# Hybrid decoder trunk on one core: more background steps between gates, row sums and their matmuls, finer steps in the S5 set-up, and four PSUM copies put first

## The chip, the cores and the metric

The kernel runs on one core of one Trainium2 chip. The metric is the device time of one execution in microseconds (us), lower is better. The core has a matrix engine (PE, with weight loads as a row of their own, PEld), a vector engine (DVE), a scalar engine (ACT), a general engine (POOL) and a queue engine that issues most transfers (SP). Each works through its own list of instructions in order, and semaphores hold an instruction until what it needs is there.

## What is computed

One layer: a wide input projection, three token mixers on parts of its columns, an output projection, and a layer norm over the residual. All is float32, 1024 tokens of width 2048.

```python
h = jnp.einsum('bld,dn->bln', x, w_in[l])
(s5_u, s5_z, ml_qk, ml_v, ml_i, ml_f, ml_o, ml_z, ssd_xbc, ssd_dt, ssd_z) = split_in(h)
y_s5 = s5_mixer(s5_u, ...) * jax.nn.silu(s5_z)
qk = jax.nn.silu(causal_dwconv(ml_qk, ml_conv_w[l], ml_conv_b[l]))
q, k = jnp.split(qk, 2, axis=-1)
y_ml = mlstm_mixer(q, k, ml_v, ml_i + ml_i_bias[l], ml_f + ml_f_bias[l], ml_o, ml_norm_g[l]) * jax.nn.silu(ml_z)
xbc = jax.nn.silu(causal_dwconv(ssd_xbc, ssd_conv_w[l], ssd_conv_b[l]))
xs, bs, cs = jnp.split(xbc, [SSD_WIDTH, SSD_WIDTH + SSD_GROUPS * SSD_STATE], axis=-1)
y = ssd_mixer(xs, bs, cs, ssd_dt, ssd_dt_bias[l], ssd_a_log[l], ssd_d[l])
y_ssd = rms_norm(y * jax.nn.silu(ssd_z), ssd_norm_g[l])
out = jnp.einsum('bln,nd->bld', jnp.concatenate([y_s5, y_ml, y_ssd], axis=-1), w_out[l])
x = layer_norm(DEEPNORM_ALPHA * x + out, ln_g[l], ln_b[l])
```

The mixers are an S5 state space model (32 groups of 64 complex states), an mLSTM with 4 heads, and a Mamba-2 SSD with 12 heads.

## The kernel before

**Matmuls.** Every float32 product of the projections is made of three passes: each operand is split (`split`, lines 170 to 172) into a high part, cast by ACT, and the rest, subtracted by DVE; PE then multiplies high by high, high by low and low by high into one PSUM bank. A weight block is called w0, w1, ... in the order of use; the class `Weights` loads the next block, and splits it, one block ahead of its use.

**Stages.** `block()` (lines 1284 to 1456) makes the columns that need no convolution, with a Strassen scheme of seven products: first the token-major products (84 units of 24 matmuls, in the stages (1), (2), (5,6), (3,7), (4)), then 35 column-major ones, then the S5 gate. Its evacuations add products up on DVE and apply Sigmoid and Silu on ACT (`put_t`, lines 1254 to 1273). Then `half(h)` runs for tokens 0 to 511 and 512 to 1023: six tiles `qk`, seven tiles `xbc` of the first SSD group pair, three more, and four last ones that are computed side by side in four PSUM banks over eight weight blocks (lines 1518 to 1535). A tile of `qk` or `xbc` is 48 matmuls in two weight blocks (`proj_c`, lines 290 to 303). Each finished tile goes through `conv` (lines 353 to 362): ACT copies the PSUM bank into a staging tile (two buffers), POOL handles the three tokens of halo, DVE makes four multiply-adds, ACT applies Silu. `outproj(h)` follows for both halves, with four PSUM banks per block of 512 columns.

**Background.** All other work is written as Python generators that stand in one queue, `Background` (lines 138 to 165). The projection loops call `bg.tick()` after each weight block; a tick adds the rate of the generator at the head of the queue to an account, and for each whole unit in it the generator is run on to its next `yield`. So a `yield` more means a step more until what follows it is written into the program, and a rate of 2.0 means two steps per tick. `bg.finish(gen)` runs a generator to its end at once. The generators that the change touches:

- `s5_setup` (lines 749 to 1028), the constants of the S5 mixer, spread over the 84 units of the token-major stage at 0.31 steps per tick, and 0.46 from stage (3,7) on (line 1408). Its loop over eight `sb` makes `lb` and `ob` (six DVE operations), then `ta` (three) and, for the `sb` before, `read_out`: four transposes and a few small matmuls on PE, a copy on ACT.
- `pre` in `half` (lines 1484 to 1493): `gates` (some 20 small DVE operations and an Exp), `cumulate` (lines 393 to 415: 14 small matmuls of `LC` with a triangle or the identity, and four ACT copies), then `ml_gates` (lines 584 to 610: a scan over time on DVE, two row transfers, transposes `mt` on PE).
- `ssd_finish` (lines 558 to 581): products with the gate, squares and their sum `sm`, a matmul `ms` of `sm` with a matrix of 1/768, the root, and the results to DRAM.
- `ml_mix`, `ml_finish` and `ssd_super` are not edited, but stand in the queue behind `pre`. The second SSD pair and `ssd_finish` of half 0 run in half 1, ahead of that half's `pre`; those of half 1 run in the output projection of half 0.

**Order on an engine.** The program is not issued in the order in which it is written. The framework plans it once when the kernel is built: among the instructions that its own model of time holds for ready, an engine takes the one written first, and `tc.high_priority()` lets an instruction pass for one written earlier. So later work moves ahead into what the plan takes for idle time; on the chip the planned order of each engine is fixed.

Of the kernel before, what the change touches and what calls it, by code (L numbers as in the profile page):

```python
# [39 lines left out]
def hybrid_trunk(ctx: ExitStack, tc: tile.TileContext, a: dict, out: bass.AP, dbg=None):  # L40
    nc = tc.nc
    pe, act, dve, pool, sync = nc.tensor, nc.scalar, nc.vector, nc.gpsimd, nc.sync
# [13 lines left out]
    def gt(name, shape=(P, HT), dtype=F32):  # L56
        return gp.tile(list(shape), dtype, name=name, tag="g")

    def pm(name):
        return mx.tile([P, HT], F32, name=name, tag="mx")  # L60
# [34 lines left out]
    cw_s, cb_s = col("ssd_conv_w", 14), col("ssd_conv_b")  # L95
# [254 lines left out]
            bg.tick()  # L350


    def conv(ps, halo, cw, cb, t, dest, nm):
        stg = sp.tile([P, 3 + HT], F32, name=nm + "st", tag="cst")
        act.copy(out=stg[:, 3:], in_=ps)
        pool.tensor_copy(out=stg[:, 0:3], in_=halo[:, t, :])
        pool.tensor_copy(out=halo[:, t, :], in_=stg[:, HT:HT + 3])
        c = gt(nm + "cv")
        dve.tensor_scalar(out=c, in0=stg[:, 0:HT], scalar1=cw[:, t, 0:1], scalar2=cb[:, t:t + 1], op0=ALU.mult, op1=ALU.add)
        for j in range(1, 4):  # L360
            dve.scalar_tensor_tensor(out=c, in0=stg[:, j:j + HT], scalar=cw[:, t, j:j + 1], in1=c, op0=ALU.mult, op1=ALU.add)  # L361
        act.activation(out=dest, in_=c, func=AF.Silu)  # L362
# [195 lines left out]
    def ssd_finish(h, yg):  # L558
        sm = gt(f"sm{h}")
        for t in range(6):  # L560
            z = gt(f"szs{h}{t}")
            sync.dma_start(out=z, in_=szd[t * P:(t + 1) * P, h * HT:(h + 1) * HT])
            dve.tensor_mul(out=yg[t], in0=yg[t], in1=z)
            act.activation(out=z if t else sm, in_=yg[t], func=AF.Square)
            if t:
                dve.tensor_add(out=sm, in0=sm, in1=z)
            if t % 2:
                yield
        yield
        ps = pm(f"ms{h}")  # L570
        pe.matmul(ps, lhsT=ones, rhs=sm, start=True, stop=True)
        rs = gt(f"rs{h}")
        dve.tensor_scalar_add(rs, ps, EPS)
        act.activation(out=rs, in_=rs, func=AF.Sqrt)
        dve.reciprocal(rs, rs)
        yield
        for t in range(6):
            dve.scalar_tensor_tensor(out=yg[t], in0=yg[t], scalar=sg_col[:, t:t + 1], in1=rs, op0=ALU.mult, op1=ALU.mult)
            sync.dma_start(out=mixT[1280 + t * P:1280 + (t + 1) * P, h * HT:(h + 1) * HT], in_=yg[t])
            if t % 2:  # L580
                yield


    def ml_gates(h, G, NC, b, lf, ir, res):
        n = f"mg{h}"

        m = gt(n + "m", (4, HT))
        dve.tensor_tensor_scan(out=m, data0=lf, data1=ir, initial=mcar, op0=ALU.add, op1=ALU.max)
        mst = sp.tile([4, 4], F32, name=n + "mst", tag="mst")
        pool.tensor_copy(out=mst[:, 0:1], in_=mcar)  # L590
        pool.tensor_copy(out=mst[:, 1:4], in_=m[:, P - 1:3 * P:P])
        pool.tensor_copy(out=mcar, in_=m[:, HT - 1:HT])
        A = gt(n + "A", (4, HT))
        dve.tensor_tensor(out=A, in0=b, in1=m, op=ALU.subtract)
        sync.dma_start(out=rowd[h][12:16], in_=A)
        A2 = gt(n + "A2", (4, HT))
        ms = mst.unsqueeze(2).to_broadcast([4, 4, P])
        dve.tensor_tensor(out=A2.rearrange("p (c k) -> p c k", k=P), in0=A.rearrange("p (c k) -> p c k", k=P), in1=ms, op=ALU.add)
        sync.dma_start(out=rowd[h][16:20], in_=A2)

        Bj = sp.tile([P, 4, 4], F32, name=n + "Bj", tag="mBj")
        dve.tensor_tensor(out=Bj, in0=G[:, :, 16:20], in1=NC[:, :, 32:36], op=ALU.add)
        yield
        yield
        mt = pm(n + "mt")
        for c in range(4):
            pe.transpose(mt[:, 4 * c:4 * c + 4], m[:, c * P:(c + 1) * P], ident[0:4, 0:4])
        em = sp.tile([P, 16], F32, name=n + "em", tag="mem")
        act.activation(out=em, in_=mt[:, 0:16], func=AF.Exp, scale=-1.0)
        res += [Bj, em]  # L610
# [138 lines left out]
    def s5_setup():  # L749
# [28 lines left out]
        def tt(o, i, j, op, eng=dve):  # L778
            eng.tensor_tensor(out=o, in0=i, in1=j, op=op)  # L779
# [219 lines left out]
        for sb in range(8):  # L999
            g4 = slice(4 * sb, 4 * sb + 4)  # L1000
            sh = [P, 4, 8, 16]

            pv = lambda t_, lo: t_[:, lo:lo + 8, g4].rearrange("p s g -> p g s").unsqueeze(3).to_broadcast(sh)
            bv = lambda t_: t_[:, g4, :].unsqueeze(2).to_broadcast(sh)
            lb, l2 = gt(f"s5lb{sb}", sh), gt(f"s5l2{sb}", sh)
            tt(lb, pv(pdr, 1), bv(bb1), mul)
            tt(l2, pv(pds, 1), bv(bb2), mul)
            tt(lb, lb, l2, sub)
            ob, o2 = gt(f"s5ob{sb}", sh), gt(f"s5o2{sb}", sh)
            tt(ob, pv(pdr, 0), bv(c1s), mul)  # L1010
            tt(o2, pv(pdi, 0), bv(c2), mul)
            tt(ob, ob, o2, sub)
            sync.dma_start(out=s5d["O"][sb], in_=f3(ob))
            lbs[sb] = lb
            yield

            av = lambda t_: t_[:, :, g4].rearrange("p x g -> p g x").unsqueeze(3).to_broadcast(sh)
            fv = lambda t_: t_[:, :, g4].rearrange("p y g -> p g y").unsqueeze(2).to_broadcast(sh)
            ta, tb = gt(f"s5ta{sb}", sh), gt(f"s5tb{sb}", sh)
            tt(ta, av(afr), fv(f1), mul)  # L1020
            tt(tb, av(a2), fv(f2_), mul)
            tt(ta, ta, tb, add)
            sync.dma_start(out=s5d["T"][sb], in_=f3(ta))
            if sb:
                read_out(sb - 1)
            yield
# [257 lines left out]
    def block():  # L1284
# [116 lines left out]
        for sg in STAGES:  # L1401
            if sg == (2,):
                aside.append(aside_2(ops[5]))
            if sg == (5, 6):
                aside.append(aside_3())
            if sg == (3, 7):
                aside.append(aside_4())
                bg.q = [(q, 0.46) for q, _ in bg.q]
            for g in range(3):
                if sg == (5, 6):  # L1410
                    ps = {5: banks(5, g, pj), 6: banks(6, g, mx)}
                    for u in range(4):
                        w = [W.next(), W.next()]
                        for i, w_ in zip(sg, w):
                            unit(i, ops[i], g, u, ps[i], w_)
                        ahead(sg, g, 6, u)
                else:
                    for i in sg:
                        ps = banks(i, g, pj)
                        for u in range(4):  # L1420
                            if (i, g) == (1, 0):
                                first.load(u)
                            unit(i, ops[i], g, u, ps, W.next())
                            ahead(sg, g, i, u)
                if sg == (1,) and g == 0:
                    aside.append(aside_1())
# [52 lines left out]
    def half(h, X, Xn):  # L1479
# [4 lines left out]
        def pre():  # L1484
            G = Gs[:, h]
            DT, LC = gates(h, G)
            yield
            yield
            NC, b, lf, ir = cumulate(h, LC)
            gx.extend([DT, NC])  # L1490
            yield
            yield from ml_gates(h, G, NC, b, lf, ir, mlg)
        bg.add(pre(), 1.5)
        qT = [gt(f"qT{h}{i}", (96, HT)) for i in range(4)]
        kT = [gt(f"kT{h}{i}", (96, HT)) for i in range(4)]
        for t in range(6):
# [3 lines left out]
            relay(qT if t < 3 else kT, dst, t % 3)  # L1500
            bg.tick()

        def finish_conv(ps, t):
            dst = gt(f"xc{h}_{t}")
            conv(ps, halo_s, cw_s, cb_s, t, dst, f"xb{h}{t}")
            return dst

        def xbc(ts):
# [14 lines left out]
        for u in range(8):  # L1523
            wh, wl = W.next()
            order = [(q, k) for q in range(4) for k in range(2)] if u in (0, 7) else [(q, k) for k in range(2) for q in range(4)]
            for q, k in order:
                K, sl = 2 * u + k, slice(q * P, (q + 1) * P)
                x_h, x_l = X.h[u][:, k, :], X.l[u][:, k, :]
                pe.matmul(ps[q], lhsT=wh[:, k, sl], rhs=x_h, start=(K == 0), stop=False)
                pe.matmul(ps[q], lhsT=wh[:, k, sl], rhs=x_l, start=False, stop=False)  # L1530
                pe.matmul(ps[q], lhsT=wl[:, k, sl], rhs=x_h, start=False, stop=(K == 15))  # L1531
                if K == 15:
                    tiles.append(finish_conv(ps[q], ts[q]))
            Xn.load(u)
            bg.tick()
        bg.finish(mix)
# [182 lines left out]
```

## Time and profile before

| | |
|---|---|
| time before, median of 3 runs | 1612.53 us (1611.51 to 1612.76) |
| the profiled execution's own time | 1610.04 us |
| its span, first to last instruction | 1608.3 us |
| DVE busy | 1120.7 us (70%) |
| ACT busy | 658.2 us (41%) |
| POOL busy | 80.3 us (5%) |
| granted PE clock, mean | 0.994 |

Times inside the trace count from the first instruction of the profiled execution. A row of a timeline gives start, duration, engine, line, operation, what is written and read, and in brackets the idle time of the engine before it with what ended it. Matmuls overlap in the pipe: a row's duration is longer than the distance to the next row, and the distance is what a matmul costs in a full stream. So PE can be shown as busy and still lose time; where that matters, starts are compared.

### The profile page before, as it was taken

The numbers are of one execution on the slowest core, as the hardware profiler recorded it, in microseconds if no ns is written. First come the engines' busy times: TensorE is split into PE (matmuls) and PEld (weight loads), VectorE is DVE, ScalarE is ACT, GpSimd is POOL, SyncE is SP. The second block draws the span as 40 slices with busy tenths as digits, with TensorE's granted clock in tenths as the row PEclk, the third lists the DMA queues.
The fourth block names the chain that finished last, engine by engine and source line by source line (L and its number), as shares of the span: only waits on it lengthen the run. The fifth ranks groups of instructions, "written<-read, shape, count | busy, mean of one in ns | idle before, by whom it ended". The sixth has DMA issues, their size and how long they took to land. (4 is left out here: it accounts for less than half of the span.)

```text
span 1608.3 us, 21146 instructions
## 1 busy us (share of the span) xinstructions
PE 1579.1 (98%) x7688; PEld 1329.4 (83%) x7688; DVE 1120.7 (70%) x1844; ACT 658.2 (41%) x927; POOL 80.3 (5%) x183
## 2 busy tenths in 40 slices
PE   9999999999999999999999999999999999999996
PEld 7898988987988888778888888788887888888884
DVE  5678978878868786565646788685697753484348
ACT  4333242147345556543542546364354331321222
POOL 0000000000001110001100000010000000000000
PEclk9999999999999999999999999999999999999998
DMA  8988777987987768364434553452654453575345
GB/s 318 328 320 316 255 269 251 306 293 223 336 302 248 247 227 275 130 223 127 137 105 159 183 169 119 151 171 66 217 195 145 132 194 118 183 242 160 129 144 183
DMA packets 139304, 333.56 MB, mean 207 GB/s; under 512 B 24489, under 2 KB 41001, under 8 KB 139201
## 3 DMA queue, kind: packets, MB, share of 16 engines
q1 hardware_dynamic: 129792, 317.54, 59.1%
q10 hardware_dynamic: 9408, 14.68, 2.6%
q8 instruction: 60, 0.98, 0.2%
q14 instruction: 44, 0.35, 0.1%
HBM read 271.74 MB, written 57.28 MB: 205 GB/s over the span
## 5 line engine op out<-in xcount | busy, mean ns | idle before, releaser
L1297 DVE TENSOR_TENSOR e<-e,b 128x512 f32<-128x512 f32 (+1 forms) x72 | 43.9, 645 | 3.7 <-PE b L1372 3.2
L1556 DVE SCALAR_TENSOR_TENSOR r<-r,mv,ln_g 128x512 f32<-128x512 f32 x32 | 23.1, 742 | 0.0
L1557 DVE SCALAR_TENSOR_TENSOR r<-r,lrs,ln_b 128x512 f32<-128x512 f32 x32 | 23.0, 742 | 0.0
L1576 DVE BATCH_NORM_STATS2 bst<-r 128x6 f32<-128x512 f32 x32 | 20.8, 682 | 0.0
L362 ACT ACT_TABLE_LOAD x15 | 19.2, 1283 | 3.7 <-DVE qc00cv L361 3.4
L1052 POOL COPY s5m0up<-s5m0u 128x256 f32<-128x256 f32 x2 | 0.8, 398 | 316.2 <-DMA s5m0u<-s5u 316.2
L1297 DVE TENSOR_TENSOR f<-f,b1c 128x512 f32<-128x512 f32 x15 | 9.4, 682 | 8.7 <-ACT f L1350 8.7
L172 DVE TENSOR_TENSOR y1l<-y1r,y1h 128x1024 fp32r<-128x1024 f32 x8 | 9.8, 1222 | 7.5 <-ACT y1h L171 7.5
L1277 ACT ACTIVATE f<-f 128x512 f32<-128x512 f32 x20 | 12.1, 628 | 6.2 <-DVE f L1297 3.2
L171 ACT CAST y1h<-y1r 128x1024 fp32r<-128x1024 f32 x8 | 8.4, 1053 | 9.1 <-PE op03p L344 9.1
L779 DVE TENSOR_TENSOR s5small<-s5small 128x32 f32<-128x32 f32 (+2 forms) x66 | 11.2, 195 | 0.7
L1548 ACT ACTIVATE lrs<-lrs 128x1 f32<-128x1 f32 x8 | 1.6, 202 | 24.4 <-DVE lrs L1547 24.4
L1297 DVE TENSOR_TENSOR f<-f,b2c 128x512 f32<-128x512 f32 x5 | 3.4, 687 | 11.6 <-PE b2c L1444 11.6
L172 DVE TENSOR_TENSOR y0l<-y0r,y0h 128x1024 fp32r<-128x1024 f32 x8 | 9.8, 1221 | 2.3 <-ACT y0h L171 2.2
L172 DVE TENSOR_TENSOR x1l<-x1r,x1h 128x1024 fp32r<-128x1024 f32 x8 | 9.8, 1219 | 2.3 <-ACT x1h L171 2.3
L731 DVE TENSOR_TENSOR sgo<-sgo,mzs 128x384 f32<-128x384 f32 x16 | 8.9, 555 | 2.3 <-DMA mzs<-zg 2.1
L171 ACT CAST y0h<-y0r 128x1024 fp32r<-128x1024 f32 x8 | 8.4, 1046 | 4.9 <-PE xbc_13p L1531 4.8
L1271 ACT ACT_TABLE_LOAD x8 | 10.3, 1283 | 0.1
L1270 ACT ACT_TABLE_LOAD x7 | 9.0, 1283 | 2.4 <-ACT e L1271 2.4
L1305 ACT COPY e<-b 128x512 f32<-128x512 f32 (+1 forms) x12 | 6.7, 558 | 7.5 <-PE b L1372 7.5
L1160 DVE TENSOR_TENSOR gsg<-gsg,gsz 128x512 f32<-128x512 f32 x8 | 5.5, 683 | 6.0 <-DMA gsz<-s5z 6.0
L741 PEld LDWEIGHTS mf<-ident,sgo 128*128 128x128 f32 x48 | 5.7, 140 | 4.7 <-DVE sgo L731 3.8
(4696 smaller groups left out, 5741.1 us busy)
## 6 DMA issues: line engine op xcount, KB each, us to landing
xn<-in_x_dram SPq DMA_DIRECT2D x32, 256.0 KB, 5.5
out_dram<-r SPq DMA_DIRECT2D x32, 256.0 KB, 3.8
x1r<-in_xT_dram SPq DMA_DIRECT2D x8, 512.0 KB, 4.3
y0r<-mixT SPq DMA_DIRECT2D x8, 512.0 KB, 3.3
y1r<-mixT SPq DMA_DIRECT2D x8, 512.0 KB, 3.5
vd<-e SPq DMA_DIRECT2D x16, 192.0 KB, 4.0
szd<-f ACTq DMA_DIRECT2D x12, 256.0 KB, 3.0
vx<-vd SPq DMA_DIRECT2D x8, 384.0 KB, 4.3
```

What stands on the lines that cost most here:

```text
L171: act.copy(out=th, in_=raw)
L172: dve.tensor_sub(out=tl, in0=raw, in1=th.bitcast(F32))
L362: act.activation(out=dest, in_=c, func=AF.Silu)
L731: dve.tensor_mul(out=sg, in0=sg, in1=sz)
L779: eng.tensor_tensor(out=o, in0=i, in1=j, op=op)
L1270: act.activation(out=c[:, 0:256], in_=c[:, 0:256], func=AF.Silu)
L1271: act.activation(out=c[:, 256:512], in_=c[:, 256:512], func=AF.Sigmoid)
L1277: act.activation(out=c, in_=c, func=AF.Silu)
L1297: dve.tensor_tensor(out=o, in0=x, in1=y, op=op)
L1556: dve.scalar_tensor_tensor(out=o, in0=o, scalar=mv[:, 0:1], in1=lng[nb], op0=ALU.subtract, op1=ALU.mult)
L1557: dve.scalar_tensor_tensor(out=o, in0=o, scalar=rs, in1=lnb[nb], op0=ALU.mult, op1=ALU.add)
L1576: dve.bn_stats(out=st[t][:, nb, :], in_=r[t][nb])
```

## The change

`conv` can put its PSUM copy first, and does so for the last four tiles of a half. `ssd_finish` has two more yields between the sum of squares and the matmul `ms`; `ml_gates` one more after the row transfers; `pre` five instead of two between `gates` and `cumulate`, at a rate of 1.8 instead of 1.5. The loop of `s5_setup` yields four times per `sb` instead of twice, and runs at 0.95 instead of 0.46 steps per tick from stage (3,7) on.

```diff
-    def conv(ps, halo, cw, cb, t, dest, nm):
+    def conv(ps, halo, cw, cb, t, dest, nm, soon=False):
         stg = sp.tile([P, 3 + HT], F32, name=nm + "st", tag="cst")
-        act.copy(out=stg[:, 3:], in_=ps)
+        with tc.high_priority() if soon else nullcontext():
+            act.copy(out=stg[:, 3:], in_=ps)
         pool.tensor_copy(out=stg[:, 0:3], in_=halo[:, t, :])
...
             if t % 2:
                 yield
         yield
+        yield
+        yield
         ps = pm(f"ms{h}")
         pe.matmul(ps, lhsT=ones, rhs=sm, start=True, stop=True)
...
         sync.dma_start(out=rowd[h][16:20], in_=A2)
+        yield

         Bj = sp.tile([P, 4, 4], F32, name=n + "Bj", tag="mBj")
...
             tt(lb, lb, l2, sub)
+            yield
             ob, o2 = gt(f"s5ob{sb}", sh), gt(f"s5o2{sb}", sh)
             tt(ob, pv(pdr, 0), bv(c1s), mul)
...
             sync.dma_start(out=s5d["T"][sb], in_=f3(ta))
+            yield
             if sb:
                 read_out(sb - 1)
             yield
...
             if sg == (3, 7):
                 aside.append(aside_4())
-                bg.q = [(q, 0.46) for q, _ in bg.q]
+                bg.q = [(q, 0.95) for q, _ in bg.q]
...
             DT, LC = gates(h, G)
-            yield
-            yield
+            for _ in range(5):
+                yield
             NC, b, lf, ir = cumulate(h, LC)
             gx.extend([DT, NC])
             yield
             yield from ml_gates(h, G, NC, b, lf, ir, mlg)
-        bg.add(pre(), 1.5)
+        bg.add(pre(), 1.8)
...
-        def finish_conv(ps, t):
+        def finish_conv(ps, t, soon=False):
             dst = gt(f"xc{h}_{t}")
-            conv(ps, halo_s, cw_s, cb_s, t, dst, f"xb{h}{t}")
+            conv(ps, halo_s, cw_s, cb_s, t, dst, f"xb{h}{t}", soon)
             return dst
...
                 if K == 15:
-                    tiles.append(finish_conv(ps[q], ts[q]))
+                    tiles.append(finish_conv(ps[q], ts[q], True))
             Xn.load(u)
```

## The prediction, made before the changed kernel ran

> **What bounds the kernel now.** I read the page first, then the waits of PE, then the clock and the instructions around each wait.
>
> ```profile
> span 1608.3 us, 21146 instructions
> PE 1579.1 (98%) x7688; PEld 1329.4 (83%) x7688; DVE 1120.7 (70%) x1844; ACT 658.2 (41%) x927; POOL 80.3 (5%) x183
> ```
>
> PE is the bound: 98% busy, so 1608.3 - 1579.1 = 29 us of the span are without it. The change touches no matmul of the projections, so all it can give is time in which PE waits, and all it can cost is new waits. PE's waits, longest first:
>
> ```profile
> PE cu0cs L397 <- DVE gt1f L378: 1.9, 1, 1.9
> PE b L1370 <- ACT w70h L171: 1.8, 1, 1.8
> PE b L1371 <- DVE w70l L172: 1.7, 1, 1.7
> ...
> PE ms L571 <- DVE sm L566: 1.2, 1, 1.2
> PE op00p L343 <- ACT xb113st L355: 1.1, 1, 1.1
> ...
> PE mg0mt L607 <- DVE mg0m L588: 0.3, 1, 0.3
> ```
>
> Each edit has its wait here: the steps in `pre` that of cu0cs, the S5 set-up the two of w70, `ssd_finish` that of ms, the early copies that of op00p, the step in `ml_gates` that of mg0mt. Together 8.0 us. One of them costs more than its wait:
>
> ```profile
> 367.50:371.00 3.50, 1.76 (x14) 1.46 (x13) 2.23 (x4) 3.09 (x6) 0.00 (x0) 1.00 0.34 115
> 371.00:371.70 0.70, 0.62 (x3) 0.53 (x4) 0.70 (x2) 0.70 (x2) 0.00 (x0) 1.00 0.93 181
> 371.80:372.60 0.80, 0.78 (x3) 0.05 (x1) 0.80 (x2) 0.80 (x2) 0.00 (x0) 0.50 1.12 323
> 374.20:378.00 3.80, 3.74 (x9) 2.97 (x10) 3.80 (x6) 0.58 (x1) 0.00 (x0) 0.50 0.81 258
> 378.00:380.00 2.00, 2.00 (x9) 1.63 (x8) 2.00 (x3) 0.00 (x0) 0.00 (x0) 0.85 1.00 287
> 1340.00:1360.00 20.00, 20.00 (x90) 16.54 (x89) 4.00 (x4) 4.22 (x4) 0.00 (x0) 1.00 0.32 106
> ```
>
> These are windows: length, then PE, PEld, DVE, ACT and POOL busy, the granted clock, DMA. An undisturbed window holds 90 matmuls in 20 us, a step of 0.22 to 0.23 us. After 3.5 us in which PE was busy for 1.76, the clock falls to 0.50 from 371.7 until about 378.6 (0.85 over the last 2 us is 0.6 us at half), some 6.9 us. Half of that is lost, less what is waited anyway. So the w70 place costs 1.8 + 1.7 and, in the 6.9 - 1.7 us of half speed, 2.6 more: 6.1 us.
>
> **The steps in `pre`.**
>
> ```profile
> 707.91 0.39 PE L300 MATMUL qk_0p<-p23h,w124l 128*128 128x512 f32 x1
> 709.88 0.20 DVE L389 TENSOR_TENSOR gt0LC<-gt0DT,nega 128x48 f32<-128x48 f32 x1
> 710.19 0.48 PE L397 MATMUL cu0cs<-gt0LC,tri 128*128 128x144 f32 x2 [1.89 <-DVE gt1f L378]
> ```
>
> cu0cs stands right behind tile qk_0, and its input LC is finished by DVE only at 710.08. Start to start 2.28 us, less a step of 0.23: 2.05 lost. The old queue runs `gates` at the first tick of the half and `cumulate` at the second. The new one, at 1.8 and with five yields, reaches `cumulate` at the fourth, behind tile qk_1: 48 matmuls of 0.227 = 10.9 us later. LC is then ready by far, and qk_1 fills PE meanwhile, its weights being loaded. I take the whole 2.05. At worst (the plan pulls cu0cs forward again, as it pulled the other half's gates forward: gt1f at 710 belongs to half 1) it is 0. Hidden from the end: the mLSTM in half 0 starts at the thirteenth tick either way.
>
> **The step in `ml_gates`.** `cumulate` and the transposes mt stand two ticks apart before (second and fourth) and after (fourth and sixth); between them come the same ACT copies behind the same Silu of a `qk` tile. I take 0 of the 0.3; the whole of it at best.
>
> **The S5 set-up.** From stage (3,7) on the loop made two steps of 0.46 per tick and now makes four at 0.95, so it runs equally fast: one `sb` in 4.3 ticks against 4.2, no step moved by more than two ticks, and it still ends before its stage. What changes is which DVE operations stand together at w70:
>
> ```profile
> 354.44 0.42 ACT L1270 ACTIVATE e<-e 128x256 f32<-128x256 f32 x1 [2.34 <-issue]
> ...
> 367.73 0.42 ACT L1271 ACTIVATE e<-e 128x256 f32<-128x256 f32 x1
> ...
> 369.98 1.05 ACT L171 CAST w70h<-w70r 128x1024 fp32r<-128x1024 f32 x1
> ```
>
> ```profile
> 370.65 0.69 DVE L779 TENSOR_TENSOR s5l<-s5small,s5bb 128x512 f32<-128x512 f32 x1
> 371.25 0.69 DVE L779 TENSOR_TENSOR s5ob<-s5small,s5c1s 128x512 f32<-128x512 f32 x1
> 371.86 1.22 DVE L172 TENSOR_TENSOR p43l<-p43r,p43h 128x1024 fp32r<-128x1024 f32 x1
> 372.99 1.22 DVE L172 TENSOR_TENSOR w70l<-w70r,w70h 128x1024 fp32r<-128x1024 f32 x1
> ```
>
> The first wait is ACT's: eight activations with a table load between each two, 354.44 to 368.15, stand ahead of the cast w70h, which ends at 371.03. The change edits none of that. The second is DVE's: the split w70l stands behind s5l and s5ob. With a yield between `lb` and `ob`, s5ob is written one tick later and falls behind the splits; w70l starts 371.86 - 371.25 = 0.61 earlier. I take 0.61. The clock fell at 371.7, ahead of the second wait (372.6), so the first one alone brought it, and I leave the 2.6 us. Ends: 6.1 gained if the first wait goes; as much lost if such a place arises once more.
>
> **The row sums.**
>
> ```profile
> 1042.22 1.10 PE L571 MATMUL ms<-sm,ones 128*128 128x512 f32 x2 [1.23 <-DVE sm L566]
> 1306.38 0.39 PE L344 MATMUL op01p<-w214l,y0h 128*128 128x512 f32 x1
> 1306.86 1.10 PE L571 MATMUL ms<-sm,ones 128*128 128x512 f32 x2
> ```
>
> Half 0: two more steps at a rate of 2.0 are one tick. ms was written behind the first weight block of qk_5 and is now written behind the second. But in the trace it ran 22 matmuls into xbc_0 (it lies between matmuls of that tile), later than either place: the plan held it until it thought sm ready, 1.2 us too early. That error stays; I take 0, between -1.2 and +1.2. Half 1: 0.48 start to start less 0.23 is 0.25; ms there gets a tick more distance from its last squares, and I take 0.25.
>
> **The copies put first.**
>
> ```profile
> 1227.17 1.28 ACT L362 ACT_TABLE_LOAD   x1
> ...
> 1232.70 0.63 ACT L362 ACTIVATE xc<-xb19cv 128x512 f32<-128x512 f32 x1 [3.14 <-DVE xb19cv L361]
> 1233.24 0.57 ACT L355 COPY xb113st<-xbc_13p 128x512 f32<-128x512 f32 x1
> 1230.35 2.32 DVE L361 SCALAR_TENSOR_TENSOR xb19cv<-xb19st,cols,xb19cv 128x512 f32<-128x512 f32 x3
> 1233.86 0.50 PE L343 MATMUL op00p<-w203h,y0h 128*128 128x512 f32 x1 [1.12 <-ACT xb113st L355]
> ```
>
> PE waits for the fourth bank, emptied by the copy of xb113 at 1233.24. There are two staging tiles, so this fourth copy needs the second one, free when DVE ends xb19cv at 1232.67. Going first, the copy passes only the Silu: 1232.70 instead of 1233.24, 0.54 us. The rest is DVE's and stays. In half 0 no bank is waited for at this place: 0.
>
> **Sum:** 2.05 + 0 + 0.61 + 0.25 + 0.54 = 3.45 us. The profiled execution took 1610.04 (span 1608.3), which gives 1606.6 for it; the median 1612.53 lies 2.5 above, and the forecast is 1612.53 - 3.45 = **1609.1**.
>
> **Rivals.**
>
> *The clock stays up.* If readouts or copies of the set-up move so that w70h comes early enough, both waits and the half clock go: 6.1 instead of 0.61, 1609.1 - 5.5 = 1603.6. For it: finer pieces around just this place, the readout copies among them. Against: the eight activations alone end at 368.15, later than PE's last matmul of w69.
>
> *The waits only move.* From the first altered step on, the whole plan is made anew. Each wait in the list is the plan's error against the chip by 1 to 2 us, and two or three new ones eat 3.45: 1612.5, give or take 2.
>
> *Slower: the passage from half 1 to the output projection.* The queue of half 1 gets later: one tick from `ssd_finish`, and `pre` needs ten steps at 1.8 (5.6 ticks) where it needed six at 1.5 (4 ticks). Counted through, `ml_mix` starts three ticks later, `ml_finish` and the second `ssd_super` two, that is 11 us, since a tile of 10.9 us has two ticks.
>
> ```profile
> 1224.72 1.09 PE L508 MATMUL s10y<-s10A,s10dx 128*64 128x128 f32 x16
> ...
> 1228.37 0.50 PE L343 MATMUL op00p<-w203h,y0h 128*128 128x512 f32 x1
> ```
>
> Now 1228.37 - 1224.72 = 3.65 us of SSD matmuls cover the convolutions between the last `xbc` matmul and op00. Two ticks later they stand inside op00: PE needs the fourth bank at 1233.86 - 1.12 - 3.65 = 1229.1 and gets it at 1233.3, a wait of 4.2 us in place of 1.1, and the clock halves, which cost 2.6 at w70. That is 3.1 + 2.6 = 5.7 more, against 2.9 gained elsewhere: 1615.3. It decides once PE runs dry for about 1.8 us, as at w70. For it: the cover goes by count. Against: the plan sees a full bank and may put the same SSD matmuls, if ready, into the gap. An early copy could add to it, since ACT's order is fixed (3.14 us idle above, in front of a Silu) and what stands behind a copy that waits for its staging tile waits too.
>
> The Trainium skill (TensorE: Matmul & The Clock Gate, Part 1) says that the clock is halved after at least one idle window of about 3.4 us. By that rule a wait of 1.8 us, such as the one before 371.08, would not halve it, and the passage would cost its wait alone, some 1612.7. The row of 367.5 to 371 speaks against it: PE was busy for half of that stretch, with the transposes of a readout among it, and the clock fell all the same. No run here shows where the limit lies.
>
> **How the numbers follow.** Forecast 0.42 (1607 to 1611: the copy's 0.54 and the 0.61 may fail, the 1.2 of ms may go); clock up 0.18 (1602 to 1605); waits moved 0.22 (1610.5 to 1614.5); slower 0.18 (1614 to 1618). A difference of 0.2%, 3.2 us, is about what a measurement of this kernel can tell from none, so faster means below 1609.3: 0.25 of the forecast and 0.18 make 0.43; same gets 0.17 + 0.20 = 0.37; slower 0.20. Range 1602 to 1615.5: it holds the first three cases and part of the fourth.
>
> **What would show it.** Right: no wait at cu0cs, with `cumulate` behind qk_1; the Silu chain still ahead of w70h, clock at 0.50 for one stretch near 372; ms in half 0 still waiting for sm; the fourth copy in front of a Silu and ending by DVE's staging release. Wrong: a granted clock of 1.00 throughout after the start, or a second stretch of 0.50, at 1225 to 1240 above all, or waits of PE for a staging copy in the last `xbc` tiles of half 1.

## The result, and the profile after

The changed kernel takes **1620.65 us** (median of 7 runs, 1616.5 to 1627.16); the kernel before took 1611.51 on the same chip (7 runs, 1610.3 to 1613.04). The ratio is 1.0061, 95% interval 1.0039 to 1.0082: slower, and above the forecast range. The profiled execution is the median one, 1620.65 us.

The head of the page of the changed kernel:

```profile
span 1618.9 us, 21166 instructions
...
PE 1579.1 (98%) x7688; PEld 1330.6 (82%) x7688; DVE 1121.7 (69%) x1844; ACT 661.9 (41%) x929; POOL 87.9 (5%) x183
```

PE is busy for as long as before, 1579.1 us, and the span is 10.6 us longer: PE stands still for that much more. PE's waits in the changed kernel (engine, instruction, what released it: total, times, longest):

```profile
PE s5m6U L1064 <- POOL s5m5X L1092: 6.1, 1, 6.1
PE mf L745 <- DVE sgo L735: 3.5, 5, 1.0
PE b L1377 <- DVE w74l L172: 2.7, 1, 2.7
PE b L1377 <- DVE w70l L172: 2.0, 1, 2.0
PE ms L574 <- DVE sm L567: 1.9, 1, 1.9
PE b L1376 <- ACT w70h L171: 1.7, 1, 1.7
...
PE op00p L343 <- ACT xb113st L356: 0.9, 1, 0.9
```

cu0cs and mg0mt are gone from the list, as forecast for the one, and as the best case for the other. Both waits of w70 are still there. But three waits are new or much longer: s5m6U, the transposes of the S5 batch s5m6 (none before); w74l, the split of weight block w74 (0.2 before); and mf, the transposes of `ml_finish` (0.3 before). That of ms rose from 1.2 to 1.9. The first is the largest of the whole kernel, and the clock falls to half within it. The same stretches by the windows, first after, then before (length, PE, PEld, DVE, ACT, POOL busy, granted clock, DMA share, GB/s):

```profile
577.00:583.00 6.00, 0.00 (x0) 0.00 (x0) 5.44 (x7) 2.09 (x2) 5.67 (x3) 0.71 0.83 285
583.00:587.00 4.00, 3.90 (x13) 3.30 (x14) 0.00 (x0) 0.69 (x2) 1.42 (x6) 0.58 0.50 138
```

```profile
577.00:583.00 6.00, 6.00 (x31) 4.93 (x31) 6.00 (x7) 3.08 (x4) 0.97 (x2) 1.00 0.62 181
583.00:587.00 4.00, 4.00 (x27) 3.48 (x26) 3.86 (x7) 1.80 (x4) 0.11 (x1) 1.00 0.95 341
```

Six microseconds without a matmul, then 13 matmuls where 27 had run.

To set runs beside one another I add up **lost time**: the distance from the start of one matmul to the start of the next, less the median distance for that shape in the kernel before. It holds waits and half clock alike. The table gives, for one profiled execution of each kernel, what was lost in a stretch of the span beyond the kernel before:

| stretch (us) | after | set-up only | gates only | sums only | copies only | after, fraction kept | before, fraction 0.27 |
|---|---|---|---|---|---|---|---|
| w70 and w74 (360 to 415) | +2.6 | +3.9 | +0.2 | +0.2 | +0.5 | +4.9 | +1.6 |
| S5 mixing, with s5m6U (415 to 700) | +7.6 | +3.1 | 0.0 | +0.7 | +0.1 | +0.3 | +8.5 |
| gates and s01 (700 to 745, 910 to 1010) | -4.8 | -0.1 | -4.6 | -1.1 | +0.9 | -4.9 | -1.3 |
| mf, half 0 (745 to 910) | +1.6 | +0.7 | +1.0 | +0.1 | -0.1 | +1.2 | 0.0 |
| ms, half 0 (1010 to 1080) | +1.3 | -0.2 | +0.2 | +0.3 | +4.8 | +1.0 | +0.1 |
| mf, half 1 (1080 to 1205) | +3.4 | +0.3 | -0.6 | +2.0 | +0.5 | +1.7 | +0.4 |
| op00 (1205 to 1260) | -0.5 | +0.2 | -0.5 | +0.1 | -1.2 | +0.1 | -0.7 |

The stretches are wide enough that a shift of 10 us between kernels moves no such place out of its row. The column "after" adds up to 11.2 us, against 10.6 of the span; the small rest lies at both ends. Each column is one execution, and executions differ: in the kernels "gates only", "sums only", "copies only" and "before, fraction 0.27", PE's order is that of the kernel before up to 467 us or further, and yet the row of w70 reads +0.2 to +1.6 there, and the time ahead of 360 us, which is not in the table, +1.4 to +3.1. So a difference of 1 to 2 us in one cell proves nothing by itself.

**How s5m6U came to wait.** SP's timeline of the changed kernel (start, duration, engine, line, what is loaded), and that of the kernel before:

```profile
561.53 0.33 SPq L209 DMA_DIRECT2D w104r<-cg  x1
569.80 0.33 SPq L209 DMA_DIRECT2D w104q<-in_w_c_dram  x1
571.54 0.32 SPq L209 DMA_DIRECT2D w105r<-cg  x1
571.91 0.98 SPq L1055 DMA_DIRECT2D s5m6u<-s5u  x2
```

```profile
558.57 0.33 SPq L209 DMA_DIRECT2D w104r<-cg  x1
558.94 0.98 SPq L1049 DMA_DIRECT2D s5m6u<-s5u  x2
568.66 0.34 SPq L209 DMA_DIRECT2D w104q<-in_w_c_dram  x1
```

SP issues in a fixed order, and w104q waits some 8 us there for its buffer. The input of the S5 batch s5m6 stood in front of it; now it stands behind it and behind w105r, and is issued 13 us later (3 of these are the whole stretch, since w104r goes out 3 us later as well). Its consumer is a pair of copies on GpSimd. They are the second half of the story. Tile s5m6u in the changed kernel (durations min, median, max in ns; first and last start), and VectorE's timeline around them:

```profile
L1058 POOL COPY s5m6up<-s5m6u x2: 398/2884/5371, 577.3 to 582.6; 128x256 f32<-128x256 f32 x2
```

```profile
577.15 1.21 DVE L223 TENSOR_TENSOR w104r<-w104r,w104q 128x1024 f32<-128x1024 f32 x1
...
581.23 1.22 DVE L172 TENSOR_TENSOR w103l<-w101r,w103h 128x1024 fp32r<-128x1024 f32 x1
587.13 1.28 DVE L1303 TENSOR_TENSOR f<-f,b37c 128x512 f32<-128x512 f32 x2 [4.69 <-PE b37c L1450]
```

Of two equal copies one shows 0.40 us and the other 5.37. VectorE ran six two-input operations without a gap, from 577.15 to 581.23 + 1.22 = 582.45. The first copy, begun at 577.33, ended 0.25 us behind that row, and the second then took its 0.40. (The wait list names the memset s5m5X as the releaser; it stands right behind the copies on GpSimd and ended at 583.08.) The Trainium skill (SBUF — State Buffer, SBUF: two separate sides) says that GpSimd shares a port pair with VectorE, held for a whole instruction by an operation with two SBUF inputs, so that the other blocks. The trace agrees, and shows more: the copy lasted over a row of instructions, not over one.

### The profile page after: what moved, and what is told of

The parts are those of the page before. It is cut to its first block, busy times and chain, and to the rows that moved or that the text cites. A ratio compares the mean times of both kernels' runs of the same rounds, so it can differ in the third digit from the quotient of the medians.

```text
span 1618.9 us, 21166 instructions
## 1 busy us (share of the span) xinstructions
PE 1579.1 (98%) x7688; PEld 1330.6 (82%) x7688; DVE 1121.7 (69%) x1844; ACT 661.9 (41%) x929; POOL 87.9 (5%) x183
## 4 chain that ended last, share of the span: by engine, by line
PE 83%; DVE 8%; DMA 4%; issue 2%; ACT 1%; SPq 1%; DVEq 0%; POOL 0%; ACTq 0%
PE b L1377 8%; PE b L1378 8%; PE b L1376 8%; PE op01p L343 1%; PE op01p L344 1%; PE op12p L345 1%; PE op12p L343 1%; PE op11p L343 1%; PE op10p L344 1%; PE op10p L343 1%; PE op03p L344 1%; PE op03p L343 1%; PE op02p L344 1%; PE op02p L343 1%; PE op11p L345 1%
## 5 line engine op out<-in xcount | busy, mean ns | idle before, releaser
L745 PE MATMUL mf<-ident,sgo 128*128 128x128 f32 x48 | 8.8, 282 | 4.3 <-DVE sgo L735 3.5
L783 DVE TENSOR_TENSOR s5small<-s5small 128x32 f32<-128x32 f32 (+2 forms) x66 | 11.2, 194 | 0.7
L1303 DVE TENSOR_TENSOR f<-f,b37c 128x512 f32<-128x512 f32 x10 | 6.5, 678 | 5.8 <-PE b37c L1450 5.8
L171 ACT CAST x1h<-x1r 128x1024 fp32r<-128x1024 f32 x8 | 8.3, 1044 | 5.1 <-PE xbc_13p L1537 5.0
```

Source lines behind the costliest of these rows:

```text
L171: act.copy(out=th, in_=raw)
L1303: dve.tensor_tensor(out=o, in0=x, in1=y, op=op)
```

## The experiments

Two pairs of theories came up one after the other, and the names in the expectations are these. First: **A**, the set-up edits cost; **B**, the later queue of half 1 costs. Then, for the set-up: **P**, the phase of the step counter, against **T**, the stage itself; for the row sums and copies: **C** and **S**.

### The parts by themselves

Each kernel is the one before with some of the diff's hunks. The set-up only:

```diff
             tt(lb, lb, l2, sub)
+            yield
...
             sync.dma_start(out=s5d["T"][sb], in_=f3(ta))
+            yield
...
-                bg.q = [(q, 0.46) for q, _ in bg.q]
+                bg.q = [(q, 0.95) for q, _ in bg.q]
```

> Only the two yields in the S5 set-up loop and the rate 0.95; the halves as before. Theory A (the loss is made in the first stages: the set-up edits rearrange the plan there, and a transfer of the S5 mixer, s5m6u, falls behind two weight loads): the two places of after come back, a wait of PE of some 6 us at s5m6U near 577 with a second stretch of half clock, and 2.7 us at w74; waits of before in the halves unchanged. From the lost time by place in the two traces, +2.5 around w70 and w74 and +7.4 between 500 and 600 us: 9 to 10 us slower than before, about 1621. Theory B (the later queue of half 1 is what costs): no more than 2 to 3 us slower, and no wait of 6 us.

Every other hunk:

> All of the change but the S5 set-up edits. Theory A: 1608 to 1613, the gate wait (2.0) and the one at mg0mt (0.4) gone, the waits of mf in half 1 (3.3) and of ms (0.7) there as in after, so that it is within 3 us of before; no second stretch of half clock. Theory B: most of the loss is here, 1616 to 1621, from waits at mf, ms and the passage to the output projection.

The gates only:

```diff
-            yield
-            yield
+            for _ in range(5):
+                yield
...
-        bg.add(pre(), 1.5)
+        bg.add(pre(), 1.8)
...
         sync.dma_start(out=rowd[h][16:20], in_=A2)
+        yield
```

> Only the steps in pre, its rate, and the step in ml_gates. Both theories: the waits at cu0cs and mg0mt go, 2.5 us. Theory A: half 1 is later by one to two ticks, small waits at mf of up to 2 us; 1609 to 1611. Theory B: slower than before by 2 us or more.

The row sums and the copies:

```diff
         yield
+        yield
+        yield
         ps = pm(f"ms{h}")
...
-                    tiles.append(finish_conv(ps[q], ts[q]))
+                    tiles.append(finish_conv(ps[q], ts[q], True))
```

> Only the two steps in ssd_finish and the four copies put first. My prediction's step: ms in half 0 still waits for sm by 1 to 2 us, the fourth copy is about 0.5 us earlier. Both theories: within 1.5 us of before, 1610 to 1613; if the queue of half 1, one tick later here, is what makes the waits at mf, they show here too, up to 2 us.

| kernel | median us | ratio to before, 95% interval |
|---|---|---|
| set-up only | 1620.46 | 1.0041 (1.0028 to 1.0053) |
| all but set-up | 1613.56 | 0.9999 (0.9989 to 1.0008) |
| gates only | 1610.54 | 0.9978 (0.9967 to 0.9990) |
| sums and copies | 1619.32 | 1.0027 (1.0016 to 1.0039) |

By these ratios the set-up costs 0.0041 x 1613 = 6.6 us, sums and copies cost 4.4, and the gates give 3.5. Together that is +7.5, and the whole change shows +9.8, within the intervals. (The other division, set-up and all but set-up, adds up to +6.5.) So the gates' step did what it was to do, and there are two separate losses. Theory A is right on the set-up, but priced it too high: 9 to 10 us were expected of it alone.

### The set-up: a fraction left in a counter

The loop's steps are given out by a counter:

```
            self.acc += self.q[0][1]
            while self.acc >= 1.0 and self.q:
                self.acc -= 1.0
```

What is left in `acc` when the set-up ends is carried into the S5 mixing. Adding up the ticks gives 0.58 with the rate 0.46 and 0.27 with 0.95. With 0.27 the step that loads s5m6u falls one tick later. Two kernels put this to the test, one line each. In the changed kernel:

```diff
         bg.finish(setup)
+        bg.acc = 0.58
```

> The whole change, with the step counter's fraction at the end of the set-up put back to the 0.58 that it had before (the finer set-up at the new rate leaves 0.27). Theory P (phase): the set-up edits cost what they do through that fraction, since it writes the load of s5m6u one tick later, behind two weight loads on SP. With 0.58 the load stands in front of w104q again, the 6.1 us wait at s5m6U and the second half-clock stretch go: 5 to 8 us less than the changed kernel's 1620.65, so 1613 to 1616. Rival T (the stage itself): the loss is made in stage (3,7), at w70 and w74, and what follows is the clock's: the time stays at 1618.5 or more.

In the kernel before:

```diff
         bg.finish(setup)
+        bg.acc = 0.27
```

> The kernel before, with one line: the step counter's fraction set to 0.27 behind the set-up, where it was 0.58. Nothing of the change is in it. Theory P: s5m6u's load falls behind w104q and w105r as in the changed kernel, a wait of 3 us or more comes up at s5m6U, and the time rises by 3 to 7 us, to 1615 to 1619. Rival T: the order of that load does not matter, the time stays within 1.5 us of the kernel before.

The changed kernel with the old fraction took 1614.71 us (1.0011, 1.0000 to 1.0023), 6 us less by the medians, and 8 less by the ratios, which compare each kernel with the kernel before of its own session. The kernel before with the new fraction and nothing else took 1619.79 (1.0043, 1.0030 to 1.0057): 6.9 us more. Its largest wait, and SP's order, are those of the changed kernel:

```profile
PE s5m6U L1058 <- POOL s5m5X L1086: 6.1, 1, 6.1
```

```profile
572.48 0.33 SPq L209 DMA_DIRECT2D w104q<-in_w_c_dram  x1
574.22 0.32 SPq L209 DMA_DIRECT2D w105r<-cg  x1
574.59 0.98 SPq L1049 DMA_DIRECT2D s5m6u<-s5u  x2
```

Theory P holds, from both sides: this largest loss has nothing to do with what the finer steps contain.

What the late load costs at its own place depends on what VectorE does beside the copies. The kernel with the set-up only has SP's new order too, and a wait of 6 us was expected of it; it waited 3.3 us and kept the full clock there. VectorE's row broke off there at 582.50, for want of a load:

```profile
583.07 1.23 DVE L223 TENSOR_TENSOR w105r<-w105r,w105q 128x1024 f32<-128x1024 f32 x1 [0.57 <-DMA w105q<-in_w_c_dram]
```

The first copy on GpSimd, begun at 580.54, took 2.22 us and ended inside this gap.

Is it the late load, or the copies that VectorE holds up? In the changed kernel, the two copies of s5m6 went to ScalarE:

```diff
-            pool.tensor_copy(out=up.rearrange("p (g s c) -> p g s c", g=4, s=8)[:, :, 4 * i:4 * i + 4, :],
+            (act.copy if n == "s5m6" else pool.tensor_copy)(out=up.rearrange("p (g s c) -> p g s c", g=4, s=8)[:, :, 4 * i:4 * i + 4, :],
```

> The whole change, but the two copies s5m6up (GpSimd: 0.40 and 5.37 us in the changed kernel, beside an unbroken row of VectorE's two-input additions) and the two of s5m7up, which read the same load, no: only those of s5m6 are done by ScalarE; SP's order is the changed kernel's, with s5m6u late. Theory K (GpSimd's copy is held up by VectorE): the two copies take about 1.3 us together on ScalarE, the wait at s5m6U falls from 6.1 to 3.5 us or less, and 2 to 5 us of the 1620.65 go. Rival L (the load alone is late): the wait at s5m6U stays above 5 us and the time within 1.5 us of the changed kernel's.

```profile
L1058 ACT COPY s5m6up<-s5m6u x2: 404/404/404, 582.9 to 583.6; 128x256 f32<-128x256 f32 x2
```

```profile
PE b L1377 <- DVE w74l L172: 2.6, 1, 2.6
...
PE s5m6U L1064 <- ACT s5m6up L1058: 1.5, 1, 1.5
```

The wait at s5m6U fell from 6.1 to 1.5 and no half clock followed there, as theory K said. Beside ScalarE's copies, too, VectorE ran a row without a gap, until 584.39. But the time did not fall: 1620.87 us (4 runs, 1.0052, 1.0038 to 1.0065), against 2 to 5 us less expected. In the profiled execution 4.9 us less were lost at s5m6U, but 2.7 more at w74 (6.83 us of half clock behind its wait, none in the changed kernel's profile), 1.2 more at w70 and 1.4 more at op00. PE came to the transposes 5.6 us later than in the changed kernel (2.7 of them from w74), and the load went out 5.4 us later, so the two stand to each other nearly as before: by an estimate from this run, some 1.5 us of the wait belong to the late load, and the rest to the copies on GpSimd. What that is worth in the whole time it does not show.

At **w70**, where the prediction looked, VectorE's order in the changed kernel is what it was, s5ob and then the splits:

```profile
370.48 0.68 DVE L783 TENSOR_TENSOR s5ob<-s5small,s5c1s 128x512 f32<-128x512 f32 x1
...
372.22 1.22 DVE L172 TENSOR_TENSOR w70l<-w70r,w70h 128x1024 fp32r<-128x1024 f32 x1
```

The other loss in the set-up's own stage is at **w74**. VectorE's timeline and SP's row of w78q, after and then before:

```profile
400.93 1.00 DVE L223 TENSOR_TENSOR w78r<-w78r,w78q 128x808 f32<-128x808 f32 x1 [4.47 <-DMA w78q<-in_w_gv_dram]
401.85 1.22 DVE L172 TENSOR_TENSOR w74l<-w74r,w74h 128x1024 fp32r<-128x1024 f32 x1
395.88 0.33 SPq L209 DMA_DIRECT2D w78q<-in_w_gv_dram  x1
```

```profile
399.01 1.00 DVE L223 TENSOR_TENSOR w78r<-w78r,w78q 128x808 f32<-128x808 f32 x1 [1.74 <-DMA w78q<-in_w_gv_dram]
399.93 1.22 DVE L172 TENSOR_TENSOR w74l<-w74r,w74h 128x1024 fp32r<-128x1024 f32 x1
394.47 0.33 SPq L209 DMA_DIRECT2D w78q<-in_w_gv_dram  x1
```

The split w74l stands behind w78r's addition, and that waits for the load w78q. In both kernels the load is issued 0.03 us after VectorE has ended w77r's addition. In the changed kernel the products s5ta and s5tb stand ahead of that addition, it starts at 394.85 instead of 393.45, the load goes out 1.4 us later, and VectorE stands still for 4.47 us, for the last two of them with the split ready behind it. The wait grew by 2.5 us: besides the 1.4, the load itself took 0.5 longer, and PE was there 0.6 earlier. To tell steps from rate I ran the steps alone:

```diff
             tt(lb, lb, l2, sub)
+            yield
...
             sync.dma_start(out=s5d["T"][sb], in_=f3(ta))
+            yield
```

> The two further steps of the S5 set-up alone, at the old rate of 0.46, which leaves the step counter's fraction at 0.58; SP has s5m6u's load in front of w104q. Theory R (the new rate costs, the finer steps do not): the wait at w74l is that of the kernel before (0.7 us or less), no wait above 1 us at s5m6U, and the time lies within 2 us of the kernel before. Rival Y (the steps themselves put set-up work of VectorE ahead of w77r and so delay w78q and w74l): w74l waits 2 us or more, and the time rises by 2 to 5 us.

1623.71 us (1.0073, 1.0058 to 1.0089): both theories missed the time. (At w74 the split w74l waited 0.5 us, as R had it, but the cast w74h ahead of it 2.3.) At 0.46 steps per tick twice as many steps do not get done before the stage ends, and `bg.finish` writes the rest in one piece. VectorE then has a block of set-up work, unbroken from 457.34 to 470.27 us, of which these are the first and the last row, and the splits of the first column-major products behind it:

```profile
457.34 0.68 DVE L779 TENSOR_TENSOR s5lb<-s5small,s5bb 128x512 f32<-128x512 f32 x1
...
470.05 0.22 DVE L779 TENSOR_TENSOR s5kb<-s5K,s5dd 128x64 f32<-128x64 f32 x1
470.19 1.22 DVE L172 TENSOR_TENSOR w86l<-w84r,w86h 128x1024 fp32r<-128x1024 f32 x1
```

```profile
PE b37c L1444 <- ACT w96h L171: 3.4, 1, 3.4
PE b6c L1446 <- DVE w86l L172: 2.4, 1, 2.4
```

From 415 to 570 us 18.1 us were lost, against 1.7 before. So the rate had to go up with the steps, and w74's delay is read from the trace only; no run sets it apart.

### The row sums and the copies

The two yields of the sums alone, then the copies alone:

```diff
         yield
+        yield
+        yield
         ps = pm(f"ms{h}")
```

> Only the two more steps ahead of the row-sum matmul. In this build SP's order of the szs loads is that of the kernel before (four ahead of w179r). Theory C (the copies cost, through SP's order): ms waits no longer than before (1.4 us or less at its place in half 0), and the time is within 1.5 us of the kernel before. Rival S (the sums cost): ms in half 0 waits 2 us or more, with a half-clock stretch behind it, and the time rises by 3 to 4.5 us as in the run of both edits.

```diff
-                    tiles.append(finish_conv(ps[q], ts[q]))
+                    tiles.append(finish_conv(ps[q], ts[q], True))
```

> Only the copies put first. In this build one szs load stands ahead of the next, three later, two behind w179r, as in the run of both edits. Theory C: ms in half 0 waits 3 us or more, op00p's wait is 0.3 or less, and the time rises by 2 to 4.5 us. Rival S: the copies take op00p's wait (1.3 to 0.3) and cost nothing else: 1 to 2 us less than the kernel before.

And each of the two in half 1 only:

```diff
-                    tiles.append(finish_conv(ps[q], ts[q]))
+                    tiles.append(finish_conv(ps[q], ts[q], h == 1))
```

> Copies put first in half 1 only; nothing else of the change. SP's order of the szs loads in half 0 is that of the kernel before (four ahead of w179r). Theory C2 (the copies cost through half 0 alone, where they move the szs loads, and half 0 has no bank to gain): op00p's wait of 1.28 us falls to 0.3, ms in half 0 waits 1.6 us or less, and the time is 0 to 2 us below the kernel before. Rival: the copies disturb elsewhere as well, the time is 1 us or more above the kernel before.

```diff
         yield
+        for _ in range(2 * h):
+            yield
         ps = pm(f"ms{h}")
```

> The two more steps ahead of the row-sum matmul in half 1 only. Theory H (the sums cost through half 0, where they shift the steps that follow and with them the mf transposes of half 1): lost time between 1080 and 1205 us is that of the kernel before (1.8 us, give or take 0.7; 3.8 with the steps in both halves), and the time is within 1 us of the kernel before. Rival: the cost is in half 1's own step, the time rises by 1.5 us or more.

| kernel | median us | ratio to before, 95% interval |
|---|---|---|
| sums only | 1614.96 | 1.0015 (1.0006 to 1.0023) |
| copies only | 1618.03 | 1.0036 (1.0024 to 1.0048) |
| copies, half 1 only | 1611.19 | 0.9993 (0.9981 to 1.0006) |
| sums, half 1 only | 1612.69 | 1.0005 (0.9994 to 1.0017) |

**Copies.** They took op00p's wait in half 1 (0.15 us of lost time in place of 1.28 with the copies in both halves; none to be seen with those in half 1 only). In the latter the fourth copy begins 0.09 us after VectorE ends xb19cv, at 1234.30:

```profile
1234.39 0.59 ACT L356 COPY xb113st<-xbc_13p 128x512 f32<-128x512 f32 x1 [2.44 <-DVE xb19cv L362]
```

In half 0, where there was nothing to gain, they moved the loads of szs, which `ssd_finish` multiplies by, on SP. Their rows with the copies in both halves, and then before:

```profile
1025.16 0.33 SPq L209 DMA_DIRECT2D w177r<-in_w_c_dram  x1
1025.58 1.34 SPq L563 DMA_DIRECT2D szs<-szd  x3
1036.52 0.33 SPq L209 DMA_DIRECT2D w178r<-in_w_c_dram  x1
1038.29 0.33 SPq L209 DMA_DIRECT2D w179r<-in_w_c_dram  x1
1038.71 1.01 SPq L563 DMA_DIRECT2D szs<-szd  x2
```

```profile
1014.22 1.85 SPq L562 DMA_DIRECT2D szs<-szd  x4
...
1032.91 0.87 SPq L562 DMA_DIRECT2D szs<-szd  x2
```

The last two go out 5.8 us later. Of these, 3.5 are not theirs: the whole stretch runs that much later in this execution (w176r goes out at 1017.38 against 1013.84). The other 2.3 come from three loads that now go out behind w177r: VectorE stands 4.06 us for the first of them, its split w175l, which frees the buffer of w178r, comes behind that, SP waits 9.5 us with w178r, and the last two loads stand behind it. VectorE waits for these, and ms for VectorE:

```profile
1029.80 0.69 DVE L564 TENSOR_TENSOR s00yt<-s00yt,szs 128x512 f32<-128x512 f32 x1 [4.06 <-DMA szs<-szd]
...
1045.21 1.31 DVE L564 TENSOR_TENSOR s01yt<-s01yt,szs 128x512 f32<-128x512 f32 x2 [3.75 <-DMA szs<-szd]
```

```profile
PE ms L572 <- DVE sm L567: 3.5, 1, 3.5
```

Within this wait begin 6.83 us of half clock (1047.1 to 1053.9). With the copies in half 1 alone, SP's order is the old one, and the cost is gone. Theory C was right on the copies: that they cost through half 0 is shown by the two runs, the way through the loads is read from the trace. A place behind w179r is not enough: in the version with gates and early copies below, four of the loads stand there, and ms waits 1.3 us.

**Sums.** They leave ms's wait in half 0 where it was (1.4 us; 1.2 before), so rival S is out; but they are not free, as C had it. The added loss is at mf in half 1 (+2.0 in the table). Its transposes wait for the sgo products (ended at 1151.77; the wait list names ScalarE's copy of xb13, ended at 1151.79), and in this run those wait for a load that came late:

```profile
1150.01 1.29 DVE L731 SCALAR_TENSOR_TENSOR sgo<-m1hm,m1nd,sgo 128x192 f32<-128x192 f32 x3 [2.09 <-DMA sgo<-og]
```

mf in half 1 lies between ms of half 0 and ms of half 1. With the yields in half 1 alone the stretch loses 1.8 us, the same as before, and the time is unchanged. So the sums cost through half 0: two steps more there, and every step of the queue behind them falls elsewhere. This rests on the traces, for the intervals of the two runs (1.0006 to 1.0023, 0.9994 to 1.0017) overlap; in the profiles of all six kernels with the yields in both halves the added loss at this place is there, +1.3 to +3.5 us.

### Versions that could be better

The hunks of `pre` and `ml_gates`, and the copies in half 1 only:

```diff
-            yield
-            yield
+            for _ in range(5):
+                yield
...
-        bg.add(pre(), 1.5)
+        bg.add(pre(), 1.8)
...
+        yield
...
-                    tiles.append(finish_conv(ps[q], ts[q]))
+                    tiles.append(finish_conv(ps[q], ts[q], h == 1))
```

> The gates' steps and the copies put first in half 1 only; no set-up edits, no further steps at the row sums. SP's order: s5m6u in front, two of the szs loads ahead of w179r and four behind it. Expected by theories P and C2: cu0cs' and op00p's waits gone (2.05 + 1.0), ms in half 0 waits 1.3 to 2.1 us: 1608 to 1611, below the kernel before by 1.5 to 4.5 us. Rival (any remaking of the plan costs about what it gains): within 1.5 us of the kernel before, or above it.

In addition, the row sums one tick earlier:

```diff
         bg.add(ssd_finish(h, yg), 2.0)
+        bg.acc = 2.0
```

> As the run of the gates and half 1's copies, with the step counter set forward to 2.0 behind the entry of the row sums: their steps are written one tick earlier, where the change writes their matmul a tick later, and all six szs loads stand ahead of w179r on SP. Theory Q (ms waits for the szs loads that stand behind w179r): the wait at ms in half 0 (1.23 to 4 us in the runs so far) falls to 0.5 or less, and the time is 1 to 2 us below that run, 1606.5 to 1609.5. Rival: ms waits for VectorE's other work, its wait stays at 1.2 us or more, and the time is the same.

The first took **1608.01 us** (0.9975, 0.9966 to 0.9984), below both kernels, but no better than the gates alone (0.9978). The copies' gain does not add to it: op00p waits twice here.

```profile
PE op00p L343 <- ACT xb113st L356: 1.6, 1, 1.6
...
PE op00p L343 <- ACT xb112st L356: 0.6, 1, 0.6
```

The matmuls s10y of the SSD now stand inside op00 (at 1228.28 and 1232.99); in the kernel before they stood ahead of its fourth bank's matmuls, from 1224.72 on.

The second, with all six szs loads ahead of w179r, cut ms's wait from 1.3 to 0.5 us, as expected, and took 1610.29 us (0.9994, 0.9983 to 1.0005), so no gain at all. 1.6 us more were lost at mf in half 1. This fits theory Q on what ms waits for, though the same line also moved ms itself, out of xbc_0 into qk_5; that the time follows was wrong.

## Why the prediction was wrong, by its own steps

- **The steps in `pre`: right.** cu0cs stands behind qk_1, at 728.47, and waits for nothing. The gates alone gave 3.5 us, where 2.05 was taken: mg0mt's 0.46 went as well (0 was taken), and some 2.3 us in the stretch of s01, which no step spoke of and whose cause I did not trace.
- **The S5 set-up: the step that failed.** It said that the new loop "runs equally fast", with "no step moved by more than two ticks", and took 0.61. Both phrases are true, and a single tick is what it cost: the fraction 0.27 for 0.58 put one load behind another on SP, 6 to 8 us. The step looked at one place, w70, and not at the queues that the moved steps pass. Nor did its 0.61 come at w70: s5ob was to fall "behind the splits", but it still stands ahead of w70l, as the rows above show, though by the counter it is written one tick later; why the plan left it there was not traced. w70l waits 2.0 us, 1.7 before. And 30 us further on w74l got the same fault, an addition of VectorE pushed back by set-up work.
- **The row sums: right at ms, wrong beyond it.** "That error stays" holds for the sums alone. What was not priced is that two steps in half 0 shift what follows to mf in half 1: +2.4 us by the ratio (0.0015), where the sum had -0.25. In half 1 the 0.25 is too small to be measured.
- **The copies: too small in half 1, wrong in half 0.** With the copies alone the whole wait of op00p went, 1.1 instead of 0.54. The mechanism was right: the fourth copy went in front of the Silu and waited for the staging tile alone. What came on top is that the first copy, xb18's, began 1.9 us after PE started the last matmul of its bank (copies in half 1 only), and 2.9 us before; that the change did this is not shown. In the changed kernel itself 0.9 of the 1.1 us stayed. "In half 0 no bank is waited for at this place: 0" took no gain for no effect. The copies were moved past other steps, the szs loads with them: 3.6 us lost at ms where 1.4 were before, and a half-clock stretch; +5.8 us by the ratio for copies alone.
- **The rivals.** "The waits only move" was the case that came true, with 0.22 and a price of 3.45 us for two or three new waits. Three new or grown waits it was, but of 6.1, 3.5 and 2.7 us, with half clock at the first: the "second stretch of 0.50" that was named as a sign of being wrong came, at 579.5 and not at 1225 to 1240. The range ended at 1615.5 because each was taken as an error of 1 to 2 us, the size of those in the old list, and that list does not show what a new order brings.
- **The slower rival** had the sign and not the place. At op00 the changed kernel lost 0.5 us less than before. Its mechanism is real: with gates and early copies together s10y does stand inside op00, and 0.8 + 1.8 us of lost time stand there in c2 in place of 1.3; it priced 4.2, and a half clock that did not come.

## What to carry to other kernels

A background loop that gives out steps by a fractional counter hands its remainder to the next loop. Whoever changes a rate or a number of steps should write down which loads change places on an in-order queue, everywhere behind the edit, before adding up what the edit saves at its own wait. Put a priority only where it has a wait to end: the same copies ended a wait of 1.1 us in one half and cost nearly 6 in the other. And try the parts singly: one part of this change was worth having, and the whole hid it.

## What the runs showed of the hardware

- **Half clock comes in whole units.** The stretches of half clock inside the kernels last 3.41 or 6.83 us, and the full-clock stretches between them are multiples of 3.413 too (365.226 = 107 x 3.4133 before the first). The Trainium skill (TensorE: Matmul & The Clock Gate, Part 1) speaks of a free-running 4096-cycle window; the traces agree with the grid. Its rule of a whole idle window of about 3.4 us does not hold here: at w74 half clock follows a lost 2.7 to 2.8 us in three runs (set-up only, b3 and c1).
- **The same wait may cost nothing more or 3.4 us more.** In the changed kernel's profile w74l's 2.7 us brought no half clock; nearly the same wait brought 3.41 us of it in a1 (set-up only) and b3, and 6.83 in c1. The changed kernel's seven runs fit this: a mean clock of 0.994 goes with 1616.5 to 1616.9, 0.990 with 1623.4 to 1627.2. The kernel before spread over 2.7 us beside it, but over 11.2 in 26 runs of a later set, so the spread is not the change's alone.
- **A GpSimd copy of 0.40 us took 5.37** beside an unbroken row of VectorE's two-input operations, 2.22 where the row had a gap after 2 us, and 0.40 on ScalarE in the same place.
